# Weights stationary, 256 tokens moving: a decoder trunk with its activations kept transposed

## The chip, the core and the metric

The kernel runs on one core of one Trainium2 chip. The metric is the device time of one execution in microseconds: 1275.04 us is the median of three runs (1274.9 to 1275.1). The profile is of one further execution, whose span, from the first to the last instruction, is 1273.1 us. In profile rows PE is TensorE's matmuls, PEld its weight loads, DVE is VectorE, ACT ScalarE, POOL GpSimd, and SP the engine that issues the DMAs.

## The reference

Two layers over one sequence of 256 tokens with 1024 channels, all float32:

```python
def swiglu(x, w_gate, w_up, w_down):
    return (jax.nn.silu(x @ w_gate) * (x @ w_up)) @ w_down

for l in range(DEPTH):                                     # DEPTH = 2
    x = x + 0.5 * swiglu(rms_norm(x, ffn1_norm[l]), ffn1_w_gate[l], ffn1_w_up[l], ffn1_w_down[l])   # D_FF = 2816
    h = rms_norm(x, mix_norm[l])
    proj = h @ w_in[l] + b_in[l]                           # 7176 columns
    q, k, v, f_logit, xr, gr, g_attn, g_rnn = jnp.split(proj, SPLIT_POINTS, axis=-1)
    y_attn = forgetting_attention(rms(q), rms(k), v, log_sigmoid(f_logit)) @ w_o_attn[l]   # 8 heads of 128
    xr = causal_depthwise_conv(xr, conv_w[l], conv_b[l])
    y_rnn = (rg_lru(xr, ...) * jax.nn.gelu(gr)) @ w_o_rnn[l]
    merged = sigmoid(g_attn) * y_attn + sigmoid(g_rnn) * y_rnn
    x = x + merged @ w_out[l]
    x = x + 0.5 * swiglu(rms_norm(x, ffn2_norm[l]), ffn2_w_gate[l], ffn2_w_up[l], ffn2_w_down[l])
```

The RG-LRU has two block-diagonal products of its own. Nearly all the arithmetic is in the matrices of 1024 by 1024 and 1024 by 2816.

## The kernel before, in words

**Products.** All weights pass through SBUF once, as pieces of 128 x 2048 float32 (tile `wr`, three buffers). A half of a piece, 128 x 1024, is split exactly into a high part (rounded by ScalarE) and a low part (VectorE subtracts), both of type float32r; they lie in the places W0 to W7, or in the general places R0 to R21 when those are taken. Activations are split in the same way. Each float32 product is the sum of three: high by high, high by low, low by high (`mm3`, lines 245 to 249), accumulated in one of eight PSUM banks B0 to B7.

**Who stands and who moves.** In a row such as `B<-W,xh` the operand named first moves through the array and the one named second is loaded into it. Activations are loaded, 128 tokens at a time, and weights move, 512 columns to a product. So the results leave PSUM with tokens on partitions. To be the loaded operand again they must be transposed, which TensorE does against the tile `ident`: the gated SwiGLU blocks, q, k, xr and gr (tiles S), the residual x (`ident,x`) and the merged branches (`ident,R`).

**RMSNorm.** The gain goes into the transposed activations (xh, xl). The 1/rms of a token is a column `rst`, applied as a per-partition scale when a product leaves PSUM; it is summed by ScalarE over x, and the power is POOL's.

**Stages.** In each SwiGLU, 11 groups of 512 columns (256 of gate, 256 of up) pass, and the down projection's pieces are interleaved with a delay of one group; its four accumulators hold banks through the whole SwiGLU. The mixer has 14 groups of 512 columns for q, k, v, xr, gr and the two merge gates, then two each for the projections of the attention, of the RG-LRU, and for the output.

**Order.** TensorE's program is a list of steps (`Step`; half a piece by 128 tokens). Everything else is a set of coroutines, which `run` and `work` resume between steps when a rough clock (`Clock`) says that what they read is there. Splits are issued at least `LEAD = 5` steps ahead if there is a place. `need` pushes a coroutine on, whatever the clock says, when a step cannot be written without it. The engines then execute their queues in the order written.

Of the kernel before, what the change touches and what calls it, by code (L numbers as in the profile page):

```python
# [28 lines left out]
NG = F // 256  # L29
# [3 lines left out]
PROJ = [("q", 0), ("k", 0), ("v", 0), ("q", 1), ("k", 1), ("v", 1), ("xr", 0), ("xr", 1),  # L33
        ("gr", 0), ("gr", 1), ("gA", 0), ("gA", 1), ("gR", 0), ("gR", 1)]
# columns of the per-layer parameter tile
P_G = {"ffn1": 0, "mix": 8, "ffn2": 16}
P_QN, P_KN, P_CW, P_CB, P_BA, P_BX, P_LAM, P_BXR, P_BGR, P_BV, NP_ = 24, 25, 26, 58, 66, 74, 82, 90, 98, 106, 114
# [5 lines left out]
STATS = 4  # L43
# [6 lines left out]
EARLYX = -0.4  # L50

# [5 lines left out]
class Clock:  # L57
    """roughly when each queue is free and each tile is written and last touched, in microseconds"""
# [11 lines left out]
    def cost(self, q, op, n, ins, kw):  # L70
        aps = sum(isinstance(kw.get(k), bass.AP) and kw[k].shape[-1] == 1 for k in ("scale", "bias", "scalar", "scalar1", "scalar2"))
        psum = ins and ins[0].space == bass.MemoryType.PSUM
        if q == "PE":
            two = ins[0].dtype == F32 and op == "matmul"
            return (2 if two else 1) * max((2 if two else 1) * n / 2400 + 0.003, 0.108)
# [62 lines left out]
class Queue:  # L138
    """an engine's queue, with the clock kept beside it"""
# [13 lines left out]
class Places:  # L153
    """equal tiles, given out by hand; the one that has been idle longest goes first"""
# [37 lines left out]
class Trunk:  # L192
    def __init__(self, ctx, tc, ws, x, xT, prm, wf, wbd, b_in, out):
        self.tc = tc
        self.ws, self.x_in, self.xT_in, self.prm, self.wf, self.wbd, self.b_in, self.out = (
            ws, x, xT, prm, wf, wbd, b_in, out)
# [11 lines left out]
        self.big = Places(c, lambda i, dt: self.t([128, 1036], f"R{i}", 1, dt), 22)  # L208
# [4 lines left out]
        self.n_pieces = self.s = 0  # L213
        self.hl, self.r, self.raw = {}, {}, {}
        self.phase, self.x_phase = 0, {0: 0, 1: 0}

# [14 lines left out]
    def slot(self, shape, dt=F32):  # L231
        """a 4 KB place; (tile, view)"""
# [17 lines left out]

    def split(self, hi, lo, src):
# [3 lines left out]
    def flex(self, out, in_, scale=None, bias=None):  # L255
        """in * scale + bias, on whichever of ScalarE and VectorE has it sooner"""
# [36 lines left out]
    def when(self, *aps, must=None, bank=False, after=0.0, queues=("DVE", "ACT")):  # L293
        """what a coroutine waits for: tiles by the clock, a condition, a free bank, room in the queues"""
# [23 lines left out]
    def push(self, labels=None):  # L318
        """go on with the first coroutine that may, whatever the clock says"""
# [10 lines left out]
    def piece(self):  # L330
        self.n_pieces += 1
        return 2 * (self.n_pieces - 1)
# [6 lines left out]
    def split_places(self):  # L339
        """where the halves of the next split go, if there is room"""  # L340
# [4 lines left out]
    def split_half(self, j):  # L345
        while self.loaded < self.n_pieces and self.loaded <= j // 2 + 2:
# [5 lines left out]
        if j < 4:  # L352
            for kk in range(2):
                w = slice(kk * 512, (kk + 1) * 512)
                self.first_x(2 * j + kk)
                self.split(hi[:, w], lo[:, w], raw[:, w])
        else:
            self.split(hi, lo, raw)
        self.hl[j] = hi, lo, places
        if j % 2:  # L360
            del self.raw[j // 2]

    def run(self):
# [5 lines left out]
        n = 2 * self.n_pieces  # L369
        self.loaded, j = 3, 0  # L370
        for s, st in enumerate(steps):
# [5 lines left out]
            while (j < n and first[j] - s <= AHEAD and self.split_places()  # L377
# [3 lines left out]
                j += 1  # L381
            hi, lo, places = self.hl[st.half]
# [10 lines left out]
    def new_xT(self):  # L393
        self.xh = self.t([128, 8, 256], "xh", 1, F32R)
        self.xl = self.t([128, 8, 256], "xl", 1, F32R)

    def rstd(self, ss, n, mean_of):
        """(ss / mean_of + eps) ** -0.5 on [128, n]"""
# [5 lines left out]
    def stats(self, t, phase, step=None):  # L404
        """1/rms of a token block"""
        yield self.step_at(step) if step else self.when(after=STATS)
        tl, junk = self.slot([1024])
# [222 lines left out]
    def ffn_end(self, l, name, t, st, ns):  # L630
# [8 lines left out]
        if last:  # L639
            return  # L640
# [533 lines left out]
```

## Time and profile before

| | |
|---|---|
| median of three runs | 1275.04 us |
| profiled execution, span | 1273.1 us |
| PE, matmuls | 1268.2 us busy, 5844 matmuls |
| PEld, weight loads | 1040.2 us busy, 5844 |
| DVE | 794.1 us busy, 1157 |
| ACT | 706.0 us busy, 1206 |
| POOL | 41.4 us busy, 58 |
| DMA | 235.03 MB, mean 185 GB/s |

The profile gives no time of the execution other than its span; the median run is 1.9 us longer than that span. Matmuls are pipelined: a row's own duration reaches into the next, so what one costs is read from the distance between starts. A float32 product that is not float32r shows in the trace as two matmuls, so the trace counts more of them than the program's order does.

### The profile page before, as it was taken

Reading aid. Unit: us, or ns where it says so; the run is one execution under the profiler, and the core shown is the slowest. Engines: PE = TensorE matmul, PEld = TensorE weight load, DVE = VectorE, ACT = ScalarE, POOL = GpSimd, SP = SyncE. Lnnn points to the kernel's source line nnn. Section 1 sums busy time; section 2 is a strip of 40 time slices with the busy share of each in tenths; the row PEclk is TensorE's granted clock in tenths of the full one; section 3 lists DMA queues with packets and bytes.
Section 4 is the critical chain, followed back from the end, with each engine's and each line's share of the span. In section 5 each row is a group of like instructions: output and inputs, shape, how many; then the busy total and the mean of one; then the engine's idle time right before and its main releaser. Section 6 shows DMA issues by size and latency. Waiting matters only on the chain.

```text
span 1273.1 us, 15298 instructions
## 1 busy us (share of the span) xinstructions
PE 1268.2 (100%) x5844; PEld 1040.2 (82%) x5844; DVE 794.1 (62%) x1157; ACT 706.0 (55%) x1206; POOL 41.4 (3%) x58
## 2 busy tenths in 40 slices
PE   9999999999999999999999999999999999999998
PEld 7888888888888888888888888888888888888887
DVE  6755557668678865555474455576685798744551
ACT  6644446677885564444363444475678755644440
POOL 0000001110000000000000000011100000000000
PEclk9999999999999999999999999999999999999999
DMA  8755454534456754455455455454434556645520
GB/s 334 293 189 187 179 203 141 197 110 170 143 209 212 251 199 184 180 198 170 162 198 199 175 192 188 180 181 160 174 110 162 185 214 231 224 175 196 199 99 33
DMA packets 36715, 235.03 MB, mean 185 GB/s; under 512 B 4609, under 2 KB 4769, under 8 KB 9761
## 3 DMA queue, kind: packets, MB, share of 16 engines
q1 hardware_dynamic: 36496, 233.94, 51.3%
q8 instruction: 45, 0.74, 0.2%
q14 instruction: 30, 0.24, 0.1%
q10 hardware_dynamic: 144, 0.12, 0.0%
HBM read 232.97 MB, written 1.06 MB: 184 GB/s over the span
## 4 chain that ended last, share of the span: by engine, by line
PE 99%; DMA 0%; ACT 0%; DVE 0%; issue 0%
PE B L149 99%; DMA prm<-prm 0%; DVE x L149 0%; ACT W L149 0%; ACT xh L149 0%
## 5 line engine op out<-in xcount | busy, mean ns | idle before, releaser
L149 DVE TENSOR_TENSOR W<-wr,W 128x1024 fp32r<-128x1024 f32 (+1 forms) x224 | 269.2, 1204 | 220.9 <-ACT W L149 220.3
L149 PE MATMUL B<-W,xh 128*128 128x512 f32 x1256 | 395.2, 396 | 0.2 <-ACT W L149 0.2
L149 ACT CAST W<-wr 128x1024 fp32r<-128x1024 f32 (+1 forms) x224 | 230.8, 1036 | 218.5 <-PE B L149 207.4
L149 PE MATMUL B<-R,xh 128*128 128x512 f32 x1048 | 330.0, 396 | 0.0
L149 PEld LDWEIGHTS B<-W,xh 128*128 128x128 f32 x1256 | 234.2, 189 | 49.8 <-DVE W L149 0.6
L149 DVE TENSOR_TENSOR R<-wr,R 128x1024 fp32r<-128x1024 f32 x204 | 243.7, 1221 | 36.9 <-ACT R L149 36.5
L149 PE MATMUL B<-R,R 128*128 128x512 f32 (+2 forms) x1036 | 250.7, 385 | 0.0
L149 PE MATMUL B<-W,xl 128*128 128x512 f32 x628 | 246.2, 392 | 0.0
L149 PEld LDWEIGHTS B<-R,xh 128*128 128x128 f32 x1048 | 194.7, 188 | 42.9
L149 PEld LDWEIGHTS B<-R,R 128*128 128x128 f32 x1036 | 181.1, 188 | 33.5
L149 ACT CAST R<-wr 128x1024 fp32r<-128x1024 f32 x204 | 207.1, 1050 | 0.0
L149 PE MATMUL B<-R,xl 128*128 128x512 f32 x524 | 205.9, 393 | 0.0
L149 PE MATMUL B<-W,R 128*128 128x512 f32 x756 | 187.2, 397 | 0.0
L149 PEld LDWEIGHTS B<-W,R 128*128 128x128 f32 x756 | 140.1, 188 | 31.1 <-DVE R L149 0.2
L149 ACT ACTIVATE S<-B,rst 128x256 f32<-128x256 f32 (+1 forms) x103 | 52.1, 506 | 164.0 <-PE B L149 163.4
L149 PEld LDWEIGHTS B<-W,xl 128*128 128x128 f32 x628 | 118.3, 188 | 25.7
L149 PEld LDWEIGHTS B<-R,xl 128*128 128x128 f32 x524 | 98.4, 188 | 22.9
L149 DVE SCALAR_TENSOR_TENSOR S<-B,rst,S 128x256 f32<-128x256 f32 x88 | 42.4, 482 | 111.7 <-ACT S L149 111.7
L149 ACT CAST R<-B 128x256 fp32r<-128x256 f32 (+1 forms) x96 | 37.5, 391 | 83.2 <-PE B L149 81.2
L149 DVE TENSOR_TENSOR R<-B,R 128x256 fp32r<-128x256 f32 (+1 forms) x96 | 42.6, 444 | 35.4 <-ACT R L149 35.4
L149 POOL TENSOR_TENSOR rst<-rst,mhalf 128x4 f32<-128x4 f32 (+1 forms) x28 | 31.4, 1122 | 979.4 <-DVE rst L149 971.1
L149 PE MATMUL B<-ident,S 128*128 128x128 f32 x304 | 52.0, 272 | 0.0
(107 smaller groups left out, 608.0 us busy)
## 6 DMA issues: line engine op xcount, KB each, us to landing
wr<-ws SPq DMA_DIRECT2D x210, 1024.0 KB, 4.8
bias<-b_in SPq DMA_DIRECT2D x16, 256.0 KB, 4.8
R<-cd SPq DMA_DIRECT2D x4, 512.0 KB, 4.8
R<-wbd SPq DMA_DIRECT2D x4, 512.0 KB, 5.5
wr<-ws SPq DMA_DIRECT2D x3, 512.0 KB, 7.8
R<-xT SPq DMA_DIRECT2D x4, 256.0 KB, 6.0
x<-x SPq DMA_DIRECT2D x2, 512.0 KB, 11.0
out<-x SPq DMA_DIRECT2D x4, 256.0 KB, 2.0
```

The lines of the kernel that those rows point to most:

```text
L149: return fn(*args, **kw)
```

## The change

The activations stay transposed, channels on partitions, from the input to the output: x itself is held as eight blocks of 128 channels by 256 tokens, and input and output are transposed on the host's side of the arrays. Except for q, k and v, the weights become the loaded operand (128 x 128) and the 256 tokens the moving one. High and low part of the activations lie side by side in one tile (`xs`, or a place R with two blocks). So a product `B<-xs,W` now moves 256 columns. The transposes of x, of the gated blocks, of xr, gr and of the merged branches go; those of q, k and of attention stay.

1/rms now belongs to a column of the result, so it is spread over all partitions (`rb`, 128 x 256) by a matmul of ones with a diagonal matrix, and is multiplied in on the way out of PSUM. The squares are summed over the blocks of x by ScalarE and VectorE and over partitions by a matmul with ones (`stats`).

The down projection becomes a stage of its own, behind all 22 blocks of 128 columns of gate and up; the 22 gated blocks wait in 11 places R. It goes by output block: 22 products of three into one bank, then the next. At the entry of a stage the steps are ordered so that the last block of channels comes last (products 0 to 6 of the first two result blocks, then the seventh of both). There are 21 places R instead of 22.

The diff, cut to its core:

```diff
+    def product(self, bank, wh, wl, xs, start, stop, sides=False):
...
+            self.mm3(bank[:, 0:256], wh, wl, xs[:, 0:256], xs[:, 256:512], start, stop)
...
-        self.big = Places(c, lambda i, dt: self.t([128, 1036], f"R{i}", 1, dt), 22)
+        self.big = Places(c, lambda i, dt: self.t([128, 1036], f"R{i}", 1, dt), 21)
...
+    def scale_x(self, l, norm, k):
+        g = self.prm_sb[:, l, P_G[norm] + k:P_G[norm] + k + 1]
+        hi, lo = self.xs[:, k, 0:256], self.xs[:, k, 256:512]
+        self.ACT.activation(hi, self.x[:, k], AF.Copy, scale=g)
+        self.DVE.scalar_tensor_tensor(lo, self.x[:, k], g, f32(hi), op0=ALU.mult, op1=ALU.subtract)
...
+    def stats(self, phase):
+        acc = self.acc.pop(phase)
+        yield self.when(acc, bank=True)
         pt = self.take(self.banks)
...
+        for t in range(2):
+            self.PE.matmul(pt[:, t:t + 1], acc[:, t * 128:(t + 1) * 128], self.ones[:, 0:1], start=True, stop=True)
+        r = self.rstd(pt[:, 0:2], 2, D)
         self.banks.give(pt)
+        yield self.when(r)
+        diag = self.t([128, 256], "sq", 2)
+        for t in range(2):
+            self.DVE.tensor_scalar(diag[:, t * 128:(t + 1) * 128], self.ident, r[:, t:t + 1], None, op0=ALU.mult)
+        yield self.when(diag, bank=True)
+        pt = self.take(self.banks)
+        self.PE.matmul(pt[:, 0:256], self.ones, diag, start=True, stop=True)
+        rb = self.t([128, 256], "rb", 1)
+        self.flex(rb, pt[:, 0:256])
...
+            elif f == 0:
+                order = [(0, range(4)), (0, range(4, 7)), (1, range(4)), (1, range(4, 7)), (0, range(7, 8)), (1, range(7, 8))]
...
+        for f in range(NF):
+            gu_steps(f)
+        halves = [self.half() for _ in range(NF)]
...
+        def down(half, d, blocks):
+            def fn(wh, wl):
+                for i, f in blocks:
+                    if f == 0:
+                        st["acc", d] = self.take(self.banks)
+                    self.need(lambda: ("h", f) in st, "glu", "stats", "x")
+                    w = slice(i * 128, i * 128 + 128)
+                    self.product(st["acc", d], wh[:, w], wl[:, w], st["hT", f // 2][:, f % 2], f == 0, f == NF - 1, SIDES)
...
-        self.ACT.activation(sh[:, 0], bank[:, 0:256], AF.Silu, scale=r)
-        self.DVE.scalar_tensor_tensor(sh[:, 1], bank[:, 256:512], r, sh[:, 0], op0=ALU.mult, op1=ALU.mult)
+        self.DVE.tensor_mul(g, self.total(banks[0], SIDES), self.rb[phase])
+        self.banks.give(banks[0])
+        self.ACT.activation(g, g, AF.Silu)
+        yield self.when(s2)
+        self.DVE.tensor_mul(h, self.total(banks[1], SIDES), g)
...
-        pt = self.take(self.banks)
-        p3 = self.transpose(pt, sh[:, 1])
...
+        y = self.t([128, 256], "sq", 2)
+        self.DVE.tensor_mul(y, self.total(bank, SIDES), self.rb[phase])
         self.banks.give(bank)
+        self.DVE.scalar_tensor_tensor(self.x[:, d], y, 0.5, self.x[:, d], op0=ALU.mult, op1=ALU.add)
```

Three places in the order of instructions. First TensorE in the first SwiGLU, at the group of steps where the interleaved down projection begins, before (places have numbers; what follows the underscore numbers the tile):

```order
L149 MATMUL B4_249<-W7_245,xl_110 128x512
L149 MATMUL B7_336<-W0_264,R4_222 128x512
L149 MATMUL B7_336<-W1_265,R4_222 128x512
L149 MATMUL B7_336<-W0_264,R4_222 128x512
L149 MATMUL B0_337<-W0_264,R4_222 128x512
L149 MATMUL B0_337<-W1_265,R4_222 128x512
L149 MATMUL B0_337<-W0_264,R4_222 128x512
L149 MATMUL B5_346<-ident_104,S2_313 128x128 x2
L149 MATMUL B1_338<-W0_264,R4_222 128x512
```

and where the down projection begins in the change:

```order
L151 MATMUL B2_1631<-xs_108,W4_1431 128x256 x2
L151 MATMUL B2_1631<-xs_108,W5_1432 128x256
L151 MATMUL B2_1631<-xs_108,W4_1431 128x256 x2
L151 MATMUL B2_1631<-xs_108,W5_1432 128x256
L151 MATMUL B4_1665<-R4_427,R8_1467 128x256 x2
L151 MATMUL B4_1665<-R4_427,R9_1468 128x256
L151 MATMUL B4_1665<-R4_427,R8_1467 128x256 x2
L151 MATMUL B4_1665<-R4_427,R9_1468 128x256
L151 MATMUL B4_1665<-R7_453,R8_1467 128x256 x2
```

The transposes are gone, and each product of 512 columns has become two of 256, with the weights as the second, loaded operand. R4 and R7 hold gated blocks.

Second, TensorE at the entry of the first mixer in the change, where the last steps of the first q group (B4 and B0) stand:

```order
L151 MATMUL B4_2394<-W6_2316,xs_1773 128x512
L151 MATMUL B4_2394<-W7_2317,xs_1773 128x512
L151 MATMUL B4_2394<-W6_2316,xs_1773 128x512 x2
L151 MATMUL B4_2394<-W7_2317,xs_1773 128x512
L151 MATMUL B4_2394<-W6_2316,xs_1773 128x512
L151 MATMUL B6_2478<-sq_2475,ones_104 128x256
L151 MATMUL B0_2428<-W6_2316,xs_1773 128x512
```

The product of ones with the diagonal of 1/rms (sq_2475) is new in TensorE's list; the sums over partitions stand 18 products of 512 columns ahead of it.

Third, VectorE at the same place in the change:

```order
L151 TENSOR_TENSOR R7_2425<-wr_2335,R4_2424 128x1024
L151 TENSOR_SCALAR rst_2438<-B7_2435 128x2
L151 TENSOR_TENSOR R17_2444<-wr_2369,R10_2443 128x1024
L151 TENSOR_TENSOR W4_2454<-wr_2369,W5_2453 128x1024
L151 TENSOR_TENSOR R11_2466<-wr_2412,R1_2465 128x1024
L151 TENSOR_SCALAR sq_2475<-ident_101,rst_2438 128x128 x2
L151 SCALAR_TENSOR_TENSOR S2_2482<-B4_2394,rst_2438,bias_2166 128x512
```

The three rows of 128x1024 between the mean square (rst) and the diagonal (sq) are weight splits.

More of the change, by code (lines that the diff above doesn't have):

```diff
@@ L351, in split_half @@
         raw = self.raw[j // 2][:, (j % 2) * 1024:(j % 2 + 1) * 1024]
[L352 to L358, printed above, removed]
+        self.split(hi, lo, raw)
         self.hl[j] = hi, lo, places
@@ L381, in run @@
                 j += 1
+            while st.half not in self.hl:
+                if self.split_places():
+                    self.split_half(j)
+                    j += 1
+                else:
+                    self.push()
             hi, lo, places = self.hl[st.half]
@@ new lines, in gu_steps @@
+            self.steps += [step(i, ks) for i, ks in order]
+        for f in range(NF):
+            gu_steps(f)
+        halves = [self.half() for _ in range(NF)]
+        runs = {}
+        for i in range(8 * NF):
+            d, f = divmod(i, NF)
+            runs.setdefault((halves[i // 8], d, i // 4), []).append((i % 8, f))
+        def down(half, d, blocks):
[6 more added lines that the diff above has]
+                    self.product(st["acc", d], wh[:, w], wl[:, w], st["hT", f // 2][:, f % 2], f == 0, f == NF - 1, SIDES)
+                    if d == 7 and f % 2:
+                        self.big.give(st.pop(("tile", f // 2)))
+            return Step(half, fn, [(self.ffn_end(l, name, phase, d, st), "x")] if blocks[-1][1] == NF - 1 else [])
@@ new lines, in ffn, with glu @@
+        self.steps += [down(half, d, blocks) for (half, d, _), blocks in runs.items()]
+    def glu(self, f, phase, banks, st):
+        if phase not in self.rb:
+            yield self.when(must=lambda: phase in self.rb)
+            yield self.when(self.rb[phase])
+        s2 = self.take(self.small)
+        g, h = s2[:, 0:256], s2[:, 256:512]
+        self.DVE.tensor_mul(g, self.total(banks[0], SIDES), self.rb[phase])
[3 more added lines that the diff above has]
+        self.DVE.tensor_mul(h, self.total(banks[1], SIDES), g)
+        self.banks.give(banks[1])
+        if ("hT", f // 2) not in st:
+            st["tile", f // 2], st["hT", f // 2] = self.slot([2, 512], F32R)
+        hT = st["hT", f // 2][:, f % 2]
+        yield self.when(s2)
+        self.split(hT[:, 0:256], hT[:, 256:512], h)
+        self.small.give(s2)
+        st["h", f] = True
@@ L714, in bias_row @@
     def bias_row(self, M, i):
-        rows = [i for i, (nm, _) in enumerate(PROJ) if nm in ("q", "k", "gA", "gR")]
+        rows = [i for i in range(6) if PROJ[i][0] != "v"]
         if i >= len(rows):
@@ L1045, with on_gate, out @@
-    on_gA = on_gR = gate
-    def on_ya(self, M, n, t, banks):
-        g = M["gA", n][1][:, t]
-        self.DVE.scalar_tensor_tensor(g, g, 1.0, banks[t], op0=ALU.add, op1=ALU.mult)
-        self.banks.give(banks[t])
-        if n == 1 and t == 1:
-            self.big.give(*(M["y", i, k][0] for i in range(2) for k in range(2)))
+    def on_gate(self, M, nm, d, banks):
+        n, j = divmod(d, 4)
+        def out():
+            if j == 0:
+                M[nm, n] = self.slot([4, 256])
+            return M[nm, n][1][:, j]
+        yield from self.scaled(M, d, banks, out)
+        g_t, g = M[nm, n]
+        yield self.when(g_t)
+        o = (16 if nm == "gA" else 24) + d
+        self.ACT.activation(g[:, j], g[:, j], AF.Tanh, scale=0.5, bias=self.hb[:, M["l"], o:o + 1])
+        M["tanh", nm, d] = True
@@ L1071, in on_yr @@
[L1071 to L1090 removed]
+        if d == 7:
+            self.big.give(*(M["yr", i][0] for i in range(4)))
@@ new lines, in on_yr, with on_out @@
+        yield self.when(m_t)
+        if ("mT", d // 2) not in M:
+            M["mT", d // 2] = self.slot([2, 512], F32R)
+        mT = M["mT", d // 2][1][:, d % 2]
+        self.split(mT[:, 0:256], mT[:, 256:512], m)
+        if d % 4 == 3:
+            self.big.give(m_t)
+        M["m", d] = True
+    def on_out(self, M, d, banks):
+        self.DVE.scalar_tensor_tensor(self.x[:, d], self.total(banks[d]), 0.5, self.x[:, d], op0=ALU.mult, op1=ALU.add)
+        self.banks.give(banks[d])
+        if d == 7:
+            self.big.give(*(M["mT", i][0] for i in range(4)))
+        yield from self.new_x(M["phase"] + 1, M["l"], "ffn2", d)
```

553 lines of the change are left out of this document (243 added, 310 removed).

## The prediction

> **What bounds the kernel now.** I read the engines' busy times first, then the chain of work that ended last, then the groups of matmuls, and last the timeline for the distance between starts, because a matmul's own duration overlaps its neighbours.
>
> ```profile
> span 1273.1 us, 15298 instructions
> PE 1268.2 (100%) x5844; PEld 1040.2 (82%) x5844; DVE 794.1 (62%) x1157; ACT 706.0 (55%) x1206; POOL 41.4 (3%) x58
> ```
>
> ```profile
> 5.53 1264.03 PE B L149 x5826
> 1269.56 0.02 issue
> 1269.58 0.69 DVE x L149
> ```
>
> TensorE works from 5.53 us to 1269.56 us without a break that the chain shows; VectorE and ScalarE have over a third of the span to spare. Two windows of the table by stage show the start and the first SwiGLU (window, length, then busy us and count of PE, PEld, DVE, ACT, POOL):
>
> ```profile
> 5.50:10.20 4.70, 4.67 (x10) 3.38 (x11) 2.72 (x5) 2.62 (x6) 0.00 (x0) 1.00 0.96 315
> 10.20:170.00 159.80, 159.80 (x714) 129.90 (x713) 96.05 (x116) 84.16 (x115) 1.71 (x5) 1.00 0.63 235
> ```
>
> The first ten products take 4.7 us, some 2.4 more than ten take later; from then on TensorE is busy in every microsecond. So the change is worth what it does to TensorE's own list of matmuls, plus any wait that it newly makes. In the groups (count, then busy and mean ns; the mean is a latency, not the price):
>
> ```profile
> L149 PE MATMUL B<-W,xh 128*128 128x512 f32 x1256 | 395.2, 396 | 0.2 <-ACT W L149 0.2
> L149 PE MATMUL B<-R,xh 128*128 128x512 f32 x1048 | 330.0, 396 | 0.0
> L149 PE MATMUL B<-W,xl 128*128 128x512 f32 x628 | 246.2, 392 | 0.0
> L149 PE MATMUL B<-R,R 128*128 128x512 f32 x876 | 224.9, 400 | 0.0
> L149 PE MATMUL B<-R,xl 128*128 128x512 f32 x524 | 205.9, 393 | 0.0
> L149 PE MATMUL B<-W,R 128*128 128x512 f32 x756 | 187.2, 397 | 0.0
> L149 PE MATMUL B<-ident,S 128*128 128x128 f32 x304 | 52.0, 272 | 0.0
> L149 PE MATMUL B<-ident,x 128*128 128x128 f32 x80 | 11.0, 272 | 0.0
> L149 PE MATMUL B<-ident,R 128*128 128x128 f32 x32 | 4.8, 272 | 0.0
> ```
>
> The first six rows are 5088 products with 512 columns moving; the other three are transposes. The timeline holds the prices, since both moving widths stand side by side there:
>
> ```profile
> 966.23 0.86 PE L149 MATMUL B<-R,R 128*128 128x256 f32 x6
> 966.93 0.64 PE L149 MATMUL B<-W,xh 128*128 128x512 f32 x2
> 967.41 0.40 PE L149 MATMUL B<-W,xl 128*128 128x512 f32 x1
> 967.64 0.62 PE L149 MATMUL B<-W,xh 128*128 128x512 f32 x2
> 968.10 0.39 PE L149 MATMUL B<-W,xl 128*128 128x512 f32 x1
> 968.33 0.87 PE L149 MATMUL B<-R,R 128*128 128x256 f32 x6
> 969.04 0.39 PE L149 MATMUL B<-W,xh 128*128 128x512 f32 x1
> ```
>
> Three products of 512 take 0.71 us (966.93 to 967.64) and 0.69 us (967.64 to 968.33), six of 256 take 0.70 us (966.23 to 966.93) and 0.71 us (968.33 to 969.04). The six are the RG-LRU's block-diagonal gates: weights stationary as hi and lo, 256 tokens moving, exactly the form that the change gives to nearly everything.
>
> ```profile
> 192.83 1.03 PE L149 MATMUL B<-ident,x 128*128 128x128 f32 x8
> 193.62 3.03 PE L149 MATMUL B<-R,R 128*128 128x512 f32 x12
> 196.49 0.63 PE L149 MATMUL B<-W,xh 128*128 128x512 f32 x2
> ```
>
> From 192.83 to 196.49 are 3.66 us for 8 transposes and 12 products of 512. At the 0.2305 us derived below, the 12 take 2.77 and a transpose 0.11 us.
>
> **The change, part by part.** *512-column products.* The 1264.0 us of the chain hold 470 transposes (51.7), 128 short float32r products (about 15), some 130 float32 passes and small ones of attention and the forget gates (about 22), and the start's 2.4: 1172.9 us remain for 5088, 0.2305 us each. In the new order 576 of them stay (q, k, v); the other 4512, or 1040.0 us, become 9024 products of 256 columns. The streamed columns are the same number, so only the fixed part of each instruction counts.
>
> *256-column products.* Their price decides the case. Beside the two sixes, the long runs are these:
>
> ```profile
> 208.47 0.28 PE L149 MATMUL B<-xh,wf 128*16 128x256 f32 x1
> ...
> 210.23 0.28 PE L149 MATMUL B<-xl,wf 128*8 128x256 f32 x1
> 210.35 0.60 PE L149 MATMUL B<-ident,S 128*128 128x128 f32 x4
> ```
>
> ```profile
> 960.05 1.60 PE L149 MATMUL B<-R,R 128*128 128x256 f32 x12
> 961.48 0.49 PE L149 MATMUL B<-ident,lg 128*128 128x128 f32 x3
> ```
>
> The sixteen products of the forget gates, with 8 or 16 columns to load, take 1.88 us: 0.1175 each. Twelve of the block diagonal, with full loads, take 1.43 us: 0.119 each; the sixes give 0.1167 and 0.1183. So it is bounded by 0.1167 and 0.120 (a little over the worst run). I take 0.1182, between the forget gates, which move the same normalised x as 5760 of the new products, and the block diagonal, which moves R tiles as the other 3264 do. 9024 x 0.1182 = 1066.6 us, 26.6 more than before (13 to 43).
>
> *Weight loads.* Their number doubles with the products. From the two rows below a load of 128 columns takes 188 ns and one of 16 columns 94, so 0.84 ns a column and an estimated 107 ns for the part that repeats.
>
> ```profile
> L149 PEld LDWEIGHTS B<-R,R 128*128 128x128 f32 x1036 | 181.1, 188 | 33.5
> L149 PEld LDWEIGHTS B<-xh,wf 128*16 128x16 f32 x16 | 1.5, 94 | 0.5
> ```
>
> The moving operand's 0.118 us covers 0.107, with 0.011 to spare where a 512 left 0.123. At nothing while that cover holds; without it the 9024 go to the upper bound and beyond.
>
> TensorE: Matmul & The Clock Gate in the Trainium skill (section "Back-to-back issue gap") gives N/2.4 + 2.5 ns for a warm matmul: 109 ns and 216 ns here, so doubling the instructions would cost only 2.7 ns a pair. The trace has 118 and 230.5, 8 and 7% over it; by the page the added time would be an estimated 12 us in place of 26.6.
>
> *Transposes.* The order has no transposes of x (80) or of the merged branches (32) any more, and of the 304 from S only the 64 of q and k: 352 x 0.11 = 38.7 us off TensorE. They lay on the bounding engine, so all of it counts.
>
> *RMS sums.* Six times two 1-column float32 products and one of 256 columns. Priced by attention's float32 rows:
>
> ```profile
> 258.67 0.81 PE L149 MATMUL B<-pT,R 128*128 128x256 f32 x4
> 259.32 0.60 PE L149 MATMUL B<-ident,S 128*128 128x128 f32 x4
> ```
>
> Four passes (two of 256, two of 128) in 0.65 us make 0.43 for a 256-column product of two passes; a tiny product, two passes with a full load each, is put at two transposes, 0.22. 12 x 0.22 + 6 x 0.43 = 5.2 us added.
>
> *VectorE and ScalarE.* A gated block needs three VectorE operations of 256 columns in place of two (88 more), and the squares and block ends bring some 70. The row for one:
>
> ```profile
> L149 DVE SCALAR_TENSOR_TENSOR S<-B,rst,S 128x256 f32<-128x256 f32 x88 | 42.4, 482 | 111.7 <-ACT S L149 111.7
> ```
>
> 158 x 0.48 is 76 us on VectorE's 794: 68% of the span. The weights to split per us of TensorE stay as they are, and the load on DMA with them. Cost nothing, behind TensorE; a split that came late would hold TensorE for its 1.22 us (row below) at least. The order puts splits about 7 us of TensorE work ahead of their use, as before.
>
> *New waits.* At the mixer's entry TensorE itself now needs the RMS: a float32 product on the diagonal of 1/rms stands 18 products (4.15 us) behind the sums, and VectorE has three weight splits ahead of that diagonal. Rows for its chain:
>
> ```profile
> 199.05 1.22 DVE L149 TENSOR_TENSOR R<-wr,R 128x1024 fp32r<-128x1024 f32 x1
> 200.19 0.15 DVE L149 TENSOR_SCALAR rst<-ss 128x1 f32<-128x1 f32 x1
> 200.42 1.45 POOL L149 TENSOR_TENSOR rst<-rst,mhalf 128x1 f32<-128x1 f32 x1 [178.84 <-DVE rst L149]
> ```
>
> Latency about 0.4, 0.15, three splits 3.7, two diagonals 0.6 (0.3 each, the size of the 128-column scalings): 4.9 us against 4.4, the tiny products included; the third split also hangs on a load. I take 1 us at each of two entries (0 to 2.5). Queued behind the waiting product are TensorE's remaining projections, so it is lost in full. Where a stage of xs starts (three entries to a SwiGLU), the last block of xs has 14 products of three, 5.0 us, before it is needed, and two splits ahead of it on VectorE: 0.3 us each (0 to 1). At the start one more scaling of 256 columns stands ahead of the first cast, 0.5 us, and the second pair of weight halves lands close to its use: 1 us in all (0 to 3). At the end two operations of 0.48 at most replace the last 0.69 us: 0.2. Together 4.1 us (0.2 to 11).
>
> *Sum.* 1273.1 + 26.6 - 38.7 + 5.2 + 4.1 = 1270.3 us of span. The median run, 1275.0, lies 1.9 over the span; so 1272.
>
> **Rivals.** *The load shows through.* With a load under every 0.118 us only 0.011 is left over, and a delay that a 512 swallows is paid. Place: every weights-stationary product. The point from which the case turns to slower is (1040.0 + 38.7 - 5.2 - 4.1) / 9024 = 0.1185 us, 0.3 ns over my price and below the twelve's 0.119. At 0.120 it is 16 us more: 1288. For it speaks the run of twelve; against it the sixes.
>
> *The short product is cheaper.* At the better six, 0.1167, the added time is 13 us: 1259. For it speaks that the forget gates, which move x, stay at 0.1175 over 16 products; against it the twelve. The page cited above points the same way.
>
> *New waits decide.* If the seven stage entries and the start stand at their upper bounds and a few splits fall late at some 2.3 us, the waits are 18 us in place of 4: 1286. Against it: in the trace nothing of this kind stood on the chain.
>
> *Short products do not last.* No run of them here is longer than 24 or so; were there a limit on instructions that shows only over many, say 0.125 us a product, it would be 61 us more: 1333. Nothing in the rows speaks for it.
>
> **How the numbers follow.** The forecast has 0.48, the cheaper product 0.17, the load showing through 0.22, the waits 0.10, the lasting limit 0.03. What this measurement can tell from no change is about 0.2%, or 2.6 us, so my 1272 stands just at that edge: of the forecast's own range, 1264 to 1280, half falls faster, three tenths within, two tenths slower. With the cheaper product, and the nearer ends of the rivals counted as no change, faster has 0.42, same 0.20, slower 0.38. The range for 8 in 10 takes in both prices of the product and the waits' upper end: 1258 to 1292; the forecast's own is 1264 to 1280.
>
> **What would show it.** The groups should show 3480, 2280, 2304 and some 960 products of 256 columns. Starts in a SwiGLU's first part should be 0.1175 apart, in the down projection 0.1185; more than 0.1195 in both is the first rival, under 0.117 the second. Idle time of TensorE should stand at the diagonal of 1/rms in the mixer and hardly elsewhere; over 8 us of it is the third. VectorE should be busy under 70%. I am wrong if TensorE is no longer on nearly all of the chain, or if the transposes' 38.7 us do not leave it.

## The result, and the profile after

The changed kernel takes 1284.46 us (1283.36 to 1285.19), the kernel before 1275.01 beside it: a ratio of 1.0073, with a 95% interval of 1.0058 to 1.0087. It is slower by 0.7%. The forecast was 1272 us, a little faster; the time lies in the range of 1258 to 1292, but on the other side of no change.

The head of the page of the changed kernel:

```profile
span 1283.3 us, 24052 instructions
...
PE 1269.4 (99%) x10040; PEld 1237.1 (96%) x10040; DVE 852.3 (66%) x1411; ACT 698.3 (54%) x1192; POOL 35.1 (3%) x48
...
PE 93%; DVE 2%; ACT 2%; DMA 2%; issue 1%; SPq 0%; ACTq 0%; DVEq 0%
```

Before, the chain of waits was TensorE's alone from 5.53 us on. Now 7% of it lies with other engines, and these 7% are in a few places only. The groups of matmuls (count, then busy and mean ns of one, then idle time ahead of them and what ended it):

```profile
L151 PE MATMUL B<-xs,W 128*128 128x256 f32 x3480 | 436.4, 285 | 6.0 <-ACT W L151 3.4
L151 PE MATMUL B<-xs,R 128*128 128x256 f32 x2280 | 278.7, 281 | 0.0
L151 PE MATMUL B<-R,W 128*128 128x256 f32 x2304 | 276.5, 280 | 1.7 <-DVE R L151 1.7
L151 PE MATMUL B<-R,R 128*128 128x256 f32 (+1 forms) x1024 | 130.3, 283 | 0.0
```

The counts are those of the forecast. The idle column is new: before, all six rows of products together stood at 0.2. What TensorE waited for, by the view of waits (us in total, times, longest; the fifth row, for a constant made at the very start, stood in the kernel before too):

```profile
PE B L151 <- ACT W L151: 3.4, 3, 1.7
PE B L151 <- DVE R L151: 1.7, 1, 1.7
PE B L151 <- DVE W L151: 1.6, 5, 0.7
PE B L151 <- DVE sq L151: 1.4, 3, 1.0
PE B L151 <- DVE mhalf L151: 1.1, 1, 1.1
PE B L151 <- ACT rb L151: 1.0, 1, 1.0
```

The timeline of TensorE gives the prices, from one long run and the start of the next:

```profile
352.82 33.28 PE L151 MATMUL B<-xs,W 128*128 128x256 f32 x276
385.93 31.12 PE L151 MATMUL B<-R,W 128*128 128x256 f32 x264
```

276 products that move xs take 33.11 us, 0.120 us each; the 264 that move an R tile take 31.12 less the 0.17 us by which a row outlasts the next row's start, 0.1172 each.

Adding up the distances between the ends of neighbouring matmuls in both traces, by kind, closes the account. A distance beyond the usual one of its kind counts as waiting, so time lost to a lower clock counts there too.

| us | before | after | moved | forecast |
|---|---|---|---|---|
| float32r products of 512 and 256 columns | 1187.6 | 1218.4 | +30.8 | +26.6 |
| transposes | 51.3 | 12.9 | -38.5 | -38.7 |
| RMS sums | 0 | 4.6 | +4.6 | +5.2 |
| waits after 20 us | 0.3 | 11.7 | +11.4 | +2.9 |
| the start, by subtraction | 8.2 | 9.8 | +1.6 | +1.0 |
| the other products (attention's and small ones), unchanged: what the rows leave | 22.1 | 22.1 | 0 | 0 |
| behind the last matmul | 3.6 | 3.8 | +0.2 | +0.2 |
| span | 1273.1 | 1283.3 | +10.2 | -2.8 |

Two terms carry the miss: the waits (8.5 us too few) and the price of the 256-column product (4.2 too little). The largest wait stands in the mixer of layer 1, where the products of gA's and gR's columns run short of weights. TensorE's timeline there (the first and the last row are cut at the edges of the window asked for):

```profile
1003.76 3.28 PE L151 MATMUL B<-xs,W 128*128 128x256 f32 x26
1008.76 0.61 PE L151 MATMUL B<-xs,W 128*128 128x256 f32 x2 [1.72 <-ACT W L151]
1010.02 10.24 PE L151 MATMUL B<-xs,W 128*128 128x256 f32 x62 [0.65 <-DVE W L151]
```

The timeline of ScalarE says what the weights waited for:

```profile
998.42 1.05 ACT L151 CAST W<-wr 128x1024 fp32r<-128x1024 f32 x1
1002.26 1.28 ACT L151 ACT_TABLE_LOAD   x1 [2.80 <-DVE R L151]
1003.56 2.01 ACT L151 ACTIVATE R<-R 128x1024 f32<-128x1024 f32 x2
1005.57 1.28 ACT L151 ACT_TABLE_LOAD   x1
1006.87 0.91 ACT L151 ACTIVATE R<-R,hb 128x256 f32<-128x256 f32 x2
1007.68 2.92 ACT L151 CAST W<-wr 128x1024 fp32r<-128x1024 f32 x3
```

Between the cast that starts at 998.42 and the next one at 1007.68, 9.26 us, ScalarE casts no weights. It stands idle for 2.80 us, because the RG-LRU's square root (the row of two at 1003.56) is next in its queue and VectorE has not yet made its operand (in VectorE's timeline that ends at 1002.19); a table load comes with it and another after it. Three casts are queued behind. The windows of these microseconds, and two of the kernel before at the same place (window, length, busy us and count of PE, PEld, DVE, ACT, POOL, then the granted clock, the DMA's share and its GB/s):

```profile
1005.00:1009.00 4.00, 2.28 (x20) 2.08 (x18) 0.26 (x1) 3.98 (x6) 0.00 (x0) 1.00 0.00 0
1009.00:1016.00 7.00, 6.35 (x30) 6.04 (x30) 5.88 (x8) 6.19 (x10) 0.00 (x0) 0.51 0.68 235
```

```profile
995.00:1010.00 15.00, 15.00 (x69) 12.40 (x68) 6.97 (x8) 14.79 (x21) 0.00 (x0) 1.00 0.38 125
1010.00:1030.00 20.00, 20.00 (x88) 16.20 (x87) 19.97 (x24) 10.19 (x12) 0.00 (x0) 1.00 0.59 207
```

After the gap TensorE is granted half its clock for 6.8 us (0.51 in the second window). In the kernel before ScalarE was just as full around the square root (14.79 of 15 us) and VectorE after it (19.97 of 20), and TensorE lost nothing. ScalarE's timeline of the kernel before, around the same square root:

```profile
991.55 1.06 ACT L149 CAST W<-wr 128x1024 fp32r<-128x1024 f32 x1 [1.66 <-PE B L149]
...
995.65 1.28 ACT L149 ACT_TABLE_LOAD   x1
996.94 2.01 ACT L149 ACTIVATE R<-R 128x1024 f32<-128x1024 f32 x2
998.86 1.03 ACT L149 CAST W<-wr 128x1024 fp32r<-128x1024 f32 x1
```

There the root did not wait for its operand, a cast stood right behind it, ahead of the second table load, and the casts paused for 7.31 us. So full engines alone do not make a wait; what is queued in which order does.

The Trainium skill, TensorE: Matmul & The Clock Gate (section on the HAM clock gate), has the clock fall to half after an idle window of about 3.4 us. The trace agrees in the half and in the length, two windows of 3.41, but the one gap ahead of the fall was 1.72 us long.

### The profile page after: what moved, and what is told of

It is laid out like the page before. It is cut to its first block, busy times and chain, and to the rows that moved or that the text cites. A ratio compares the mean times of both kernels' runs of the same rounds, so it can differ in the third digit from the quotient of the medians.

```text
span 1283.3 us, 24052 instructions
## 1 busy us (share of the span) xinstructions
PE 1269.4 (99%) x10040; PEld 1237.1 (96%) x10040; DVE 852.3 (66%) x1411; ACT 698.3 (54%) x1192; POOL 35.1 (3%) x48
## 3 DMA queue, kind: packets, MB, share of 16 engines
q1 hardware_dynamic: 35776, 230.79, 51.3%
## 4 chain that ended last, share of the span: by engine, by line
PE 93%; DVE 2%; ACT 2%; DMA 2%; issue 1%; SPq 0%; ACTq 0%; DVEq 0%
PE B L151 93%; DVE R L151 1%; DMA wr<-ws 1%; ACT R L151 1%; ACT W L151 1%; DVE W L151 1%; DMA x<-xT 0%; ACT L151 0%; DVE acc L151 0%; DVE sq L151 0%; SPq L151 0%; DVE x L151 0%; ACT sq L151 0%; ACT rb L151 0%; ACTq L151 0%
## 5 line engine op out<-in xcount | busy, mean ns | idle before, releaser
L151 PE MATMUL B<-xs,W 128*128 128x256 f32 x3480 | 436.4, 285 | 6.0 <-ACT W L151 3.4
L151 PEld LDWEIGHTS B<-xs,W 128*128 128x128 f32 x3480 | 426.0, 193 | 8.9 <-ACT W L151 4.1
L151 PE MATMUL B<-xs,R 128*128 128x256 f32 x2280 | 278.7, 281 | 0.0
L151 PE MATMUL B<-R,W 128*128 128x256 f32 x2304 | 276.5, 280 | 1.7 <-DVE R L151 1.7
L151 PEld LDWEIGHTS B<-R,W 128*128 128x128 f32 x2304 | 273.7, 188 | 1.9 <-DVE R L151 1.9
L151 PEld LDWEIGHTS B<-xs,R 128*128 128x128 f32 x2280 | 272.7, 189 | 0.2
L151 PE MATMUL B<-R,R 128*128 128x256 f32 (+1 forms) x1024 | 130.3, 283 | 0.0
L151 PE MATMUL B<-R,xs 128*128 128x512 f32 x336 | 85.0, 400 | 0.0
L151 PEld LDWEIGHTS B<-R,xs 128*128 128x128 f32 x336 | 61.7, 188 | 13.0
L151 PE MATMUL B<-W,xs 128*128 128x512 f32 x240 | 61.9, 399 | 0.0
L151 ACT ACTIVATE xs<-x,prm 128x256 fp32r<-128x256 f32 x48 | 23.9, 506 | 25.5 <-DVE x L151 22.1
```

The costliest lines, as they stand in the source:

```text
L151: return fn(*args, **kw)
```

## The experiments

The theory after the first reading: the doubling costs what a 256-column instruction costs anywhere; the transposes were really to be had; and the time turned because of waits that stand at a few places, mainly behind the square root in ScalarE's queue. The rivals: weights as the stationary operand are the expensive part, the transposes had been partly hidden, the engines are simply too full in the mixer.

**pairs: the doubling alone, in the kernel before.**

```diff
-        mm(out, ah, bh, start=start, stop=False)
-        mm(out, ah, bl, start=False, stop=False)
-        mm(out, al, bh, start=False, stop=stop)
+        cuts = [slice(0, 256), slice(256, 512)] if pair and n == 512 else [slice(0, n)]
+        for a, b, first, end in ((ah, bh, start, False), (ah, bl, False, False), (al, bh, False, stop)):
+            for c in cuts if not first else [slice(0, n)]:
+                mm(out[:, c], a, b[:, c], start=first, stop=end and c.stop == n)
```

> The kernel before, in which all products of 512 moving columns but those of q, k, v and the first of each accumulation are issued as two of 256: 4352 become 8704. Weights still move, nothing else is touched. If the price of a product goes by its number of columns alone, as the sum took it (0.1182 us against 0.2305), the time rises by 4352 x 0.0059 = 26 us, to 1301 (13 us at 0.1167, 41 at 0.120). If the fixed part of an instruction costs nothing when the same stationary tile is loaded twice running, it stays at 1275.

1305.93 us, ratio 1.0238 (1.0223 to 1.0253): 30.6 us more. Its TensorE timeline, with weights moving:

```profile
58.41 0.64 PE L149 MATMUL B<-R,xh 128*128 128x256 f32 x4
...
61.28 0.64 PE L149 MATMUL B<-W,xh 128*128 128x256 f32 x4
```

Between the two rows lie four groups of six, 24 products in 2.87 us: 0.1196 each. By the distances of ends the products went from 1187.6 to 1217.6 us, 6.9 ns for each one doubled; 4512 of them make 31 us, what the change itself shows. So the price is that of twice as many instructions, and that the weights became the stationary operand is not it. Loading the same stationary tile twice running saved nothing here.

**twice: each removed transpose done twice, in the kernel before.**

```diff
-        for j in range(m):
+        for j in [j for j in range(m) for _ in range(times)]:
             self.PE.transpose(pt[:, j * 128:(j + 1) * 128], src[:, j * 128:(j + 1) * 128], self.ident)
```

> The kernel before, in which each of the 352 transposes that the change removes is done twice running. If a transpose costs TensorE 0.11 us and nothing covers it, the time rises by 38.7 us, to 1314. If transposes lie partly under other work, by less; at 1290 or under, the 38.7 us of the sum were never to be had.

1312.24 us, ratio 1.0290 (1.0274 to 1.0305): 36.9 us more.

```profile
197.53 1.91 PE L149 MATMUL B<-ident,x 128*128 128x128 f32 x16
199.19 1.63 PE L149 MATMUL B<-R,R 128*128 128x512 f32 x6
```

Sixteen transposes take 1.66 us here, 0.104 each by the starts; by the ends they are 0.109 apart, and all transposes together rose by 38.5 us. Of the 38.7 us expected 36.9 show in the time, so little if anything hid them, and the change did take them away. The 1.8 us between are not explained.

**shift and pad: where xs lies.** In the changed kernel the price differs by what is moved (0.120 against 0.117). Setting the trace beside the addresses of the tiles, I found xs and all weight tiles at the same offset modulo 256 bytes, while the R tiles stand at all four multiples of 64.

```diff
 # shift
-            self.xs = self.t([128, 8, 512], "xs", 1, F32R)
+            self.xs = self.t([128, 4112], "xs", 1, F32R)[:, 16:].rearrange("p (a b) -> p a b", a=8)
 # pad
-            self.xs = self.t([128, 8, 512], "xs", 1, F32R)
+            self.xs = self.t([128, 4144], "xs", 1, F32R)[:, 0:4096].rearrange("p (a b) -> p a b", a=8)
```

> The changed kernel with the tile xs put 64 bytes further on in its partition; nothing else differs. In the changed kernel products that move xs end 119.9 ns apart, those that move an R tile 117.9. If that is the place of xs against the weight tiles, which now start at the same offset modulo 256 bytes, the distance falls to 117.8 and the time by 3480 x 0.0021 = 7 us, to 1277. If it is a property of the stage (more splits beside it), it stays at 1284.

1283.52 us, ratio 1.0067 (1.0050 to 1.0084): about 1 us less than the changed kernel, and the products of xs still 119.9 ns apart. (In its profile the clock accounts for that: half the clock lasted 3.4 us after the wait of layer 1, not 6.8.)

```profile
352.18 33.28 PE L151 MATMUL B<-xs,W 128*128 128x256 f32 x276
385.30 31.12 PE L151 MATMUL B<-R,W 128*128 128x256 f32 x264
```

That was a miss of the experiment, not of the theory: the weight tiles lie right behind xs, so the 64 bytes in front moved both, and their distance stayed 0. So shift is the control: it moves both tiles, keeps their distance, and the price stays. With the free bytes behind xs only the weight tiles (and all that lies behind them) move.

> The changed kernel with 192 bytes left free behind the tile xs, so that the weight tiles start 192 bytes off xs modulo 256; the shift of 64 bytes had moved the weight tiles along with xs and left their distance at 0. In the changed kernel an R tile loaded as weights behind a product that moves xs costs 119.4, 116.8, 117.6 and 115.8 ns at distances of 0, 64, 128 and 192 bytes; the weight tiles all stand at 0 and cost 119.9. If the distance is the cause, the 3480 products of xs fall to 115.8 ns and the time by 14 us, to 1270. If it is not, 1284.

1274.57 us, ratio 0.9996 (0.9986 to 1.0005): 9.9 us less than the changed kernel.

```profile
350.61 32.66 PE L151 MATMUL B<-xs,W 128*128 128x256 f32 x276
383.11 31.16 PE L151 MATMUL B<-R,W 128*128 128x256 f32 x264
```

The same 276 products take 32.50 us in place of 33.11; over all 3480 the mean falls from 119.87 to 116.82 ns, while those that move R stay (31.16). The rows of the loads, from the changed kernel's page and then from this one's, show where it sits: a load of W behind xs took 193 ns and takes 189, which is what a load of R took in both.

```profile
L151 PEld LDWEIGHTS B<-xs,W 128*128 128x128 f32 x3480 | 426.0, 193 | 8.9 <-ACT W L151 4.1
```

```profile
L151 PEld LDWEIGHTS B<-xs,W 128*128 128x128 f32 x3480 | 414.5, 189 | 8.5 <-ACT W L151 4.3
```

So the distance between the moving tile and the weights to be loaded is a cause. The size was 10 and not 14 us, since 115.8 was not reached, and the remaining 512-column products, whose weights move, rose from 229.7 to 233.0. Its waits came to 12.1 us, against 11.7 in the changed kernel.

**late: the square root later in ScalarE's queue.**

```diff
+            yield self.when(after=4.0, queues=("ACT",))
             for i in range(2):
                 self.ACT.activation(M["rt", i][0], M["rt", i][0], AF.Sqrt, scale=0.25)
```

> The changed kernel, in which ScalarE's square root in the mixer is put into its queue 4 us of TensorE work later. Theory: in layer 1 ScalarE reaches it 2.8 us before VectorE has its operand, and with its two table loads it holds back three weight casts; TensorE waits about 3.3 us and then runs 6.8 us at half the clock. Then these 5 to 7 us go and the time is 1278 to 1280. Rival: ScalarE is simply full there (40.6 of 45 us), the casts are late anyway and the wait only moves: 1284.

1278.85 us, ratio 1.0029 (1.0017 to 1.0040): 5.6 us less than the changed kernel. Its window at the place, and its longest wait:

```profile
1005.00:1016.00 11.00, 11.00 (x95) 11.00 (x94) 5.08 (x7) 10.96 (x20) 0.00 (x0) 1.00 0.44 143
```

```profile
PE B L151 <- DVE R L151: 1.7, 1, 1.7
```

ScalarE is still busy for 10.96 of 11 us, but TensorE is busy for all 11, at the full clock. Here the root finds its operand made, and from one cast to the next around it pass 6.1 us (999.70 to 1005.78) in place of 9.26. Not the load on ScalarE made the wait, but an instruction that waited at the head of its queue. The waits after 20 us fell from 11.7 to 6.2 us, the products kept their prices. What stays is the entry of w_o_rnn's products, where TensorE waits for VectorE's yr (the gated output of the RG-LRU, which these products read).

**lead8: the splits of weights earlier.**

```diff
-LEAD = 5
+LEAD = 8
```

> The changed kernel, in which the splits of weights are put into the queues 8 steps ahead of their use and not 5. Theory: ScalarE holds casts back for 9.3 us (from 998.42 to 1007.68) behind the square root, and 5 steps of 12 products are 7.1 us of TensorE work, 8 are 11.3: then the wait at 1005 to 1016 goes without touching the square root, and the time is 1278. Rival: places for split weights are not free that early, or ScalarE is merely full: 1284.

1284.91 us, ratio 1.0075 (1.0060 to 1.0090): nothing. The wait of 1005 to 1016 did go, as the theory had it, but others came, at the next places of the mixer:

```profile
1043.36 0.38 PE L151 MATMUL B<-R,W 128*128 128x256 f32 x1 [2.29 <-ACT R L151]
1044.78 2.52 PE L151 MATMUL B<-R,W 128*128 128x256 f32 x11 [1.04 <-DVE R L151]
```

Waits after 20 us: 11.9 us, as before. The rows fit that a longer lead puts the weights ahead of the RG-LRU in the same queues, so that TensorE then waits for the RG-LRU; that the order of the queues is the reason was not tested by itself.

**rms: the column of 1/rms alone at the mixer's entry.**

```diff
+        self.r[phase] = r
         yield self.when(r)
...
-        self.r[phase], self.rb[phase] = r, rb
+        self.rb[phase] = rb
...
-        self.need(lambda: phase in self.rb, "stats", "x")
+        self.need(lambda: phase in self.r, "stats", "x")
```

> The changed kernel, in which the projections of q, k, v wait for the column of 1/rms alone, which VectorE and GpSimd make, and no longer for its diagonal's product on TensorE. Theory: of the waits, those at the two entries to the mixer (1.23 and 0.48 us) go, since TensorE no longer has the diagonal's product put ahead of its projections: 1283. Rival: the diagonal is only waited for a little later: 1284.5.

1281.78 us, ratio 1.0052 (1.0037 to 1.0067): 2.7 us less than the changed kernel. The diagonal's product in the mixer of layer 0, first in the changed kernel, then here:

```profile
211.47 0.70 PE L151 MATMUL B<-sq,ones 128*128 128x256 f32 x2 [0.96 <-DVE sq L151]
```

```profile
212.33 0.59 PE L151 MATMUL B<-sq,ones 128*128 128x256 f32 x2
```

The wait is gone at both entries; that accounts for 1.7 us, the waits as a whole fell by 1.8. The remaining 0.9 us belong to no wait: the start is 1.2 us shorter in this trace, as it is by 1.1 in late's and 1.0 in pad's, which do not touch it either.

**mend and mend2: the three together.** mend joins pad, late and rms; in mend2 the square root comes 2 us later and not 4.

```diff
-            yield self.when(after=4.0, queues=("ACT",))
+            yield self.when(after=2.0, queues=("ACT",))
```

> The changed kernel with three of its costs taken off at once: the square root put later, the column of 1/rms alone at the mixer's entry, and the weight tiles 192 bytes off xs. If the costs add, 1284.5 - 5.6 - 1.7 - 14 = 1263. If the distance is not the cause of the 119.9 ns: 1277.

1268.51 us, ratio 0.9946 (0.9929 to 0.9962): faster than the kernel before, but 5 us short of the sum. With what pad, late and rms gave singly (9.9, 5.6 and 2.7) the sum is 1266.3; the 2.2 us that are left are the wait for yr, which with the half clock behind it grew from 2.0 us in late to 4.2. TensorE at the entry of w_o_rnn (the first row is cut at the window's edge):

```profile
1019.80 8.48 PE L151 MATMUL B<-R,W 128*128 128x256 f32 x70
1030.64 12.95 PE L151 MATMUL B<-R,W 128*128 128x256 f32 x95 [2.35 <-DVE R L151]
```

> The kernel with all three mended, but the square root put only 2 us later in place of 4. In the changed kernel ScalarE stood idle for 2.80 us before it, so 2 us should still spare the weight casts most of the wait, and the merged branches come 2 us earlier than with 4. If the wait of 4.0 us at 1030 was the price of the later root: 1264 to 1266. If any order of this kernel keeps VectorE too full there, the wait stays somewhere between 1000 and 1050: 1268 to 1270.

1273.35 us, ratio 0.9983 (0.9973 to 0.9992): worse than mend, against the expectation.

```profile
1029.48 0.38 PE L151 MATMUL B<-R,W 128*128 128x256 f32 x1 [0.76 <-ACT R L151]
1033.58 11.65 PE L151 MATMUL B<-R,W 128*128 128x256 f32 x75 [3.71 <-DVE R L151]
```

An earlier root made the wait for yr longer (3.71 against 2.35), so that wait is not the price of a later root. In both, TensorE reaches this entry some 8 us earlier than in late (1028.3 and 1028.7 against 1036.8 us), while yr comes through the queues of VectorE and ScalarE: a faster TensorE waits for it. That the RG-LRU's chain sets the pace there fits these rows; no run took work off that chain, so it is not shown.

**sides: two instructions in place of three in the SwiGLU stages.**

```diff
-SIDES = False
+SIDES = True
```

> The changed kernel, in which the products of the four SwiGLU stages are two instructions in place of three: the hi weights against hi and lo of the activations side by side (512 columns), the lo weights against hi (256). 2112 instructions fewer with the same columns; 208 additions more on VectorE and as many copies on ScalarE. If an instruction has a fixed price whichever operand is stationary: 2112 x (3 x 0.1191 - 0.2305 - 0.1185) = 17 us less, 1267. If the added additions turn into waits of TensorE, above 1275.

1268.01 us, ratio 0.9944 (0.9929 to 0.9959): the lowest median of all runs, though not to be told from mend's, and 0.56% faster than the kernel before. The head of its page, and its longest wait, which stands at the start (7.8 us):

```profile
PE 1254.9 (99%) x7928; PEld 1131.7 (89%) x7928; DVE 937.6 (74%) x1613; ACT 754.9 (60%) x1406; POOL 35.7 (3%) x48
```

```profile
PE B L151 <- DVE xs L151: 2.5, 1, 2.5
```

The total met the expectation by two errors that cancel. The products fell by 12.8 us (6.1 ns for each instruction saved, not 8), and the waits after 20 us from 11.7 to 5.5: no wait stands at the root of either layer. The edit also gives VectorE and ScalarE other work and so another order; that this is why the wait is gone was not tested. The start and the end took some of the gain back.

**sides_pad, mend_sides, sides2 and sides_all: the same with more of it.** They add pad and rms; then late as well; then, without pad, rms and the root 2 us later; and last pad and rms with the two instructions for the mixer's column products too.

```diff
-                        self.product(banks[d], wh[:, w], wl[:, w], rhs(k), k == 0, k == 7)
+                        self.product(banks[d], wh[:, w], wl[:, w], rhs(k), k == 0, k == 7, SIDES)
```

> The changed kernel with two instructions in place of three in the SwiGLU stages, with 192 bytes behind xs, and with the column of 1/rms alone at the mixer's entry. From 1268.0: 1.7 to 2.7 off for the entry, 1315 mixer products 3.05 ns cheaper (4.0 off), some 1.5 off for the 256 after a 512, and up to 2.8 on for the 512s, which are dearer at other distances than 0: 1262 to 1266. If the waits only move, 1268.

1275.32 us, ratio 0.9999 (0.9989 to 1.0008): 7 us slower than sides.

```profile
375.92 0.80 PE L151 MATMUL B<-xs,W 128*128 128x256 f32 x2 [2.19 <-ACT W L151]
...
412.57 7.69 PE L151 MATMUL B<-R,W 128*128 128x256 f32 x50 [1.78 <-DVE R L151]
```

Most of the 7 us are waits: they are back at 12.3 us, now in the mixer of layer 0, at the same two places as in layer 1 of the changed kernel: the casts of weights, then yr. Whether the bytes or the column of 1/rms shifted the order there, this run cannot say. And the bytes behind xs bring nothing here: the 256s fell by 2.6 us and the 512s rose by 3.1.

> The same with the square root put 4 us later as well. In the run with two instructions the square root cost TensorE no wait; so if the order around it stays, nothing changes against the kernel without it (1262 to 1266); if the later square root pushes the merged branches back, as it seems to have done with all three mended (a wait of 4.0 us at 1030), 2 us more.

1269.47 us, ratio 0.9956 (0.9941 to 0.9971). The later root takes away the wait for casts again (waits of 7.4 us in place of 12.3), here in layer 0; a wait for yr of 2.5 us remains. The theory of the root holds at a second place.

> The kernel with two instructions in the SwiGLU stages, without the bytes behind xs, with the column of 1/rms alone and the square root 2 us later. Theory: of the 7 us that came on when the column and the bytes were added to it, some 2 are the dearer 512s at a distance of 192 bytes, and the rest is a wait in the mixer of layer 0 (5.8 us at 375 and 3.6 at 410) that the new order made; with the root 2 us later and the distance back at 0 it is 1262 to 1266. If the order around the root is not what made that wait, 1268 or above.

1273.85 us, ratio 0.9988 (0.9979 to 0.9997). Outside the range expected. No wait for casts stands in the mixer of layer 0 any more, but the one for yr has grown to 3.7 us, as in mend2; the waits after 20 us are 9.5 us.

> The kernel with two instructions, 192 bytes behind xs and the column of 1/rms, with the two instructions also for the mixer's products (896 more): at 8 ns each 7 us less, 1256 to 1259. Rival: VectorE, which was busy for 28.5 of 30 us in the mixer of layer 1, gets 112 additions more there and TensorE waits for it: 1265 or above.

1330.80 us, ratio 1.0436 (1.0421 to 1.0452). The rival, by far more than it said.

```profile
428.94 2.90 PE L151 MATMUL B<-R,W 128*128 128x512 f32 x8 [16.07 <-DVE R L151]
```

```profile
415.00:441.00 26.00, 7.93 (x23) 6.44 (x24) 17.96 (x25) 10.82 (x19) 0.00 (x0) 0.54 0.17 61
```

The products fell by only 2.2 us against sides_pad, and the waits rose to 69 us. VectorE is idle for 8 of these 26 us, so the wait is not plain work. ScalarE's timeline has 9.46 us of idle time (to 427.45) ahead of the cast of the RG-LRU's result, which VectorE works on until then, and the next cast of weights (428.50) stands right behind it. So here, too, an instruction at the head of ScalarE's queue waits for VectorE and holds up what follows. What made VectorE so late I did not follow up.

## Why the prediction was wrong

**The bound.** Right: TensorE's own list of matmuls decides, and 93% of the chain is still TensorE's.

**The 512-column products and their number.** 0.2305 us each and the counts 3480, 2280 and 2304: right.

**The price of a 256-column product: mis-sized.** The step "I take 0.1182, between the forget gates ... and the block diagonal" made +26.6 us; it was +30.8. For the products that move R it was good (0.1179). For those that move xs I trusted the forget gates, which move the same x at 0.1175; xs against R is 0.1177, but xs against W, 3480 products, is 0.1199. The rows I read could not say it, since the forget gates load small tiles of their own. The mean of all 9024 is 0.1186, just past the 0.1185 at which the prediction's own balance turns. The sign by which I judged the first rival ("more than 0.1195 in both" parts) did not come: 0.1190 over all products that move xs, 0.1179 over those that move R, the down projection's among them. The load does show through, as this rival had it, but not under every 0.118 us: under those loaded from one distance, and pad takes it away.

**Transposes and RMS sums.** 38.5 against 38.7, and 4.6 against 5.2. Right, and confirmed by twice.

**VectorE and ScalarE, "Cost nothing, behind TensorE": this step failed.** VectorE's share was right (66% against 68%), though by luck in part: 254 operations came, not 158, but they were shorter (58 us, not 76). And a share was the wrong thing to look at. The queues of the mixer were full for tens of microseconds (14.79 of 15 and 19.97 of 20 us in the kernel before), the change gave them a new order, and I looked at neither window. I even wrote the price, "a split that came late would hold TensorE", and gave it no place, because splits stand "about 7 us of TensorE work ahead of their use". ScalarE's casts paused for 9.26 us behind the square root, longer than that lead: 5.5 us of the 11.7, the half clock included, as late shows. Whether the added operations or the new order made the root's operand late, no run separates.

**New waits at the entries.** The mixer's two entries were forecast at 1 us each and took 1.23 and 0.48; the mechanism (the diagonal's product at the head of TensorE's queue) was right, as rms shows. The SwiGLU entries after the first layer's start cost nothing, forecast 0.9. Not seen: 1.8 us at 30 us, where the products of the first SwiGLU wait for the spread 1/rms (by the row, for ScalarE's copy of it out of PSUM, so it seems for a free bank), and 1.9 us at 1046, for yr.

**The rival "new waits decide"** had 0.10 and 1286 us. Its mark, over 8 us of idle time, did not come cleanly: TensorE idles 6.4 us after the first 20 us and 10.2 over the span (1.3 before), and the 11.7 hold the half clock too. That its time came is partly luck: it reckoned with 14 us more of waits and the forecast's price of a product, and what came were 9 us more of waits and 4 for the products. Its chance was too low for the reason I gave against it: that nothing of this kind stood on the chain before. That says that the old order had no such wait, not that the order had room for another.

**The margin.** The forecast of 1272 was 3 us from no change, on a balance of +27 against -39. With both mis-sized terms on one side (13 us) the sign turned, though the time stayed inside the wide range; with either one mended the time is within 0.3% of the kernel before (pad 1274.57, late 1278.85).

**Slips in the working.** The estimate of 12 us that the prediction draws from the Trainium skill should be 11: the formula it quotes makes 2.5 ns a pair, not 2.7. The "seven stage entries" are five and the start. Neither changes the sum. The two signs by which the prediction would have been given up, TensorE off the chain and the transposes not saved, did not come.

## What to carry to other kernels

When one engine is the bound and the others have "a third to spare", look at the windows in which the others are full, and ask there what waits at the head of each queue: one operand that is late holds back everything behind it, and the bounding engine pays the delay and, after most of the long waits here, some microseconds at half the clock. A change that reorders work has to be priced with such waits from the start, since they came and went by 5 to 10 us in these runs with edits that touched nothing else. And a balance of two large opposite terms is no forecast of a sign, unless the price of the commonest instruction is known to a few tenths of a nanosecond: here one nanosecond on 9024 products is 9 us, three times the gain that was forecast.

## What was not expected of the hardware

The distance between two matmuls depends on where their operands lie. With xs moving and a tile W loaded next, 256 columns take 119.9 ns when both start at the same offset modulo 256 bytes and 116.8 at a distance of 192 (pad); R tiles loaded behind xs in the changed kernel give 119.4, 117.6, 116.8 and 115.8 at 0, 128, 64 and 192, where the loads before and after stand at the same distance. At 512 columns it is the other way round: in the kernel with two instructions xs against W takes 230.4 at 0 and 233.0 at 192. So the price of splitting a 512 in two is 9 ns at the one distance (2 x 119.9 against 230.4) and under 1 at the other (2 x 116.8 against 233.0). That the distance matters is shown by shift and pad; why is not.

A gap of 1.72 us in TensorE's work, with a smaller one behind it, was followed by 6.8 us at half the clock; one of 1.65 us at 1046 in the same run was followed by none. The first one's fall came 0.24 us after the gap had ended. The clock records of the traces show a grid: within each of the sixteen runs all changes of the clock lie whole multiples of 3.413 us apart (294 of them between two changes in the changed kernel). Cut along this grid, after the first 20 us, every full-clock stretch in which TensorE was idle for 1.78 us or more was followed by half the clock, and none with up to 1.51; of the seven between 1.64 and 1.76 three were. The two gaps above lie whole in one stretch each, on the two sides of half a stretch (1.71). That idle time within a stretch is what decides fits all these rows, but no run was made to test it.

The Trainium skill, TensorE: Matmul & The Clock Gate (section on the HAM clock gate), says that the window runs free of the kernel's start. The traces agree: the first line of the grid lies 2.07 us behind the first instruction in the changed kernel and 0.02 us behind it in the kernel before.
